# Sixty-six steps into fifty-nine: respacing the attention units of a two-layer encoder's second layer

## The chip, the core and the metric

The kernel runs on one core of a Trainium2 chip. A core has five engines that run side by side, each working through its own list of instructions in order: TensorE (PE in the profile, its weight loads as PEld), VectorE (DVE), ScalarE (ACT), GpSimd (POOL), and SyncE (SP), which here only issues DMA transfers. An instruction that needs another engine's result waits at the head of its engine's list, and all that is behind it in that list waits with it. The metric is the device time of one execution in microseconds (us); lower is better.

## What is computed

The input is `x` with 1024 rows of 1024 numbers. Two layers follow one another, and a last RMSNorm closes them. The change concerns the second layer only, differential attention with eight heads. Cut to what matters:

```python
def diff_mixer(h, ...):                       # h: 1024 x 1024, normalised rows of x
    q, k, v, gate = split(h @ w_in)           # w_in: 1024 x 4096
    # per head: q and k have 2 maps of 64, v has 128 columns
    sc = einsum('bqhcd,bkhcd->bhcqk', qb, k)  # two maps c = 0, 1
    p = softmax(sc - slopes * abs(pos_q - pos_k))
    a = p[:, :, 0] - lam * p[:, :, 1]
    o = rmsnorm(einsum('bhqk,bkhd->bqhd', a, v), head_g) * (1 - lambda_init)
    return (o * silu(gate)) @ w_o
```

All is float32. The kernel keeps that precision by splitting each operand of a product into a high and a low part in TensorE's faster float32 format; each product is then three matmuls (high by high, high by low, low by high).

## The kernel before

The second layer's attention is one loop, written out by hand: inside `tc.manual_schedule(engines=MAN)` the order of the program text is the order of every engine's list, so where a call stands in the loop decides what waits for what. Behind the loop, TensorE's and SyncE's lists stay in the text's order, and a scheduler orders the other three.

Two kinds of work are woven together in this loop.

- **Half blocks.** The projection `h @ w_in` is cut into blocks of 128 columns, named by kind and head: `V0`, `K1`, `Q1` and so on; a `G` block is a head's gate, a `W` block the V columns of two heads. `blocks` lists them in order. A block is worked off in halves of 512 rows (a `W` in four pieces); `block_mm` (lines 1156 to 1163) or `pair_mm` (1146 to 1154) issues a half's matmuls: 24 of 512 columns, or 48 of 256. Each half writes one PSUM tile `A`. Its copies out of PSUM are made by `DONE[kind]` in two portions, both taken up in the next step (`next(pend, 0)`): a high part on ACT (lines 97, 1177, 1215) and a low part on DVE (lines 1171, 1179, 1217 and 1218). A block's weights are loaded two blocks ahead, and split into high and low by a DVE cast (line 99) and a GpSimd subtraction (line 104).
- **Units.** A unit is one head and 128 of its query rows; there are 64, eight to a head. `scores` (line 1293) issues 12 matmuls into two PSUM tiles `S`, one for each softmax map. `maximum` (line 1299, on DVE) subtracts the distance bias, reads `S` for the last time and finds each row's maximum; `exp` (line 1307) runs on ACT; `ratio` and `combine` (lines 1311 to 1316, DVE) form the map `p`. One step later `transposes` (line 820) turns `p` on TensorE into two PSUM tiles `T`, and `split` copies these into a high part (line 97, ACT) and a low part (line 828, DVE). Each pair of units (a chunk) is then multiplied by V: `pv1`, 24 matmuls at line 1324, into a tile `A`. That product is copied to `ot` (line 1426, ACT), transposed into a tile `T` (`out1`, line 1330), copied from there and squared on ACT (lines 1331 and 1334).

PSUM is the scarce thing: there are two `S` tiles, two `T` tiles and two `A` tiles in all. One unit's scores fill both `S` tiles, so the next unit's scores cannot start before DVE has done both maxima of the unit before.

Each step of the loop runs in this order: scores of a new unit `nx`; the first portion of the last half block's copies; the unit's maxima and exponentials; the transposes and splits of the unit `cur` begun earlier; a half block; and then, where the step is in `DOUBLE`, a whole second unit, from scores to `combine`, with no half block behind it. Then come `out1`; up to four pieces of a head's finishing work on DVE (`finish1`: a reciprocal square root by steps on 128x8 tiles at lines 108 to 117, eight scalings at line 1348); a piece of the second layer's own modulation gate (`ada_gate`: DVE, lines 240 and 242; at its end TensorE, line 282); where the head's gate is done, `finish1b`, eight transposes at line 1358 into two `T` tiles and two DVE products at line 1360; the cast of the next block's weights; and last `pv1`, in every second step.

Before the change the loop has 66 steps, for u from -1 to 64. Each begins one unit, and those at u = 48, 51, 54 and 57 two. Each has a half block until these run out at u = 57. From u = 58 on there are units to finish and no half blocks, and in the same steps the loop loads and splits the weights of the output projection (`wo_split`: ACT high parts `woh`, GpSimd low parts `wol`) and the attention output of the first query half (`o_split`: ACT and DVE, tile `oT`); `WFILL` places output matmuls (`out_k`, lines 340 to 342) for row tiles 0 and 1 at u = 60, 61 and 62, two steps behind the splits that they need.

Of the kernel before, what the change touches and what calls it, by code (L numbers as in the profile page):

```python
# [55 lines left out]
def body(tc, x, c, positions, ada_w, ada_b, norm_g, mla_w_in, mla_q_norm_g, mla_w_q_up,  # L56
# [4 lines left out]
    with ctx:  # L61
# [1290 lines left out]
        def finish1b(h):  # L1352
# [19 lines left out]
            "V0 K1 Q1 W1 G0 K2 Q2 G1 K3 Q3 W3 G2 K4 Q4 G3 K5 Q5 W5 G4 K6 Q6 G5 K7 Q7 V7 G6 G7").split()]  # L1372
        NB = len(blocks)
        SKIP = ()
        stream, todo = {}, [(b, i) for b in range(NB) for i in range(4 if blocks[b][0] == "W" else 2)][1:]
        for u in range(-1, NU + 1):
            if u not in SKIP and todo:
                stream[u] = todo.pop(0)
# [17 lines left out]
        for u in range(-1, NU + 1):  # L1396
            n = 2 if u in DOUBLE else 1
            starts[u] = list(range(nu, nu + n))
            nu += n
        with tc.manual_schedule(engines=MAN):  # L1400
# [3 lines left out]
            for u in range(-1, NU + 1):  # L1404
                nxs = [units[v] for v in starts[u] if v < NU]
                for nx in nxs:
                    dist_load(nx.u + 2)
                b, hf = stream.get(u, (NB, 0))
                n = 4 if b < NB and blocks[b][0] == "W" else 2
                if hf == n - 1 and b + 2 < NB:  # L1410
                    kind, h = blocks[b + 2]
                    raws[b + 2] = pair_load(h) if kind == "W" else block_load(kind, h)
# [3 lines left out]
                if u < 0:  # L1416
# [4 lines left out]
                if u < 0:  # L1421
                    block_mm(ps, wq, 1, range(4, 8))
# [7 lines left out]
                cur = 0 <= u < NU  # L1430
                if cur:
                    tps = chunks[u // 2].transposes(units[u])
                for nx in nxs[:1]:
                    nx.maximum(1)
                    nx.exp(1)
                    if u < 0:
                        pend = q_done(heads[0], 1, ps)
                        next(pend)
# [3 lines left out]
                if cur:  # L1442
                    chunks[u // 2].split(units[u], tps)
                next(pend, 0)
                for k in WFILL.get(u, ()):
# [4 lines left out]
                blk = b < NB  # L1450
                if blk:
                    kind, h = blocks[b]
                    ps = A_()
                    if kind == "W":
                        pair_mm(ps, wb[b], hf)
                    else:
                        block_mm(ps, wb[b], hf, range(8))
# [13 lines left out]
                pump(fin, 4)  # L1471
                if u >= 8 and u % 2 == 0:
                    pump(gate1)
                if u in FIN:
                    pump(fin, 99)
                    finish1b(FIN[u])
                if blk:
                    pend = DONE[kind](heads[h], hf, ps)
                    if kind == "V":
                        turn = heads[h], hf  # L1480
                    if hf == n - 2 and b + 1 < NB:
                        wb[b + 1] = (pair_split if blocks[b + 1][0] == "W" else block_split)(raws[b + 1])
# [92 lines left out]
```

## Time and profile before

| | |
|---|---|
| three runs | 1637.22, 1638.22, 1638.44 us; median 1638.22 |
| profiled execution | 1639.5 us; its span, from the first to the last instruction, 1637.7 us |
| mean granted TensorE clock | 0.979 |
| busy in the span: PE, PEld, DVE, ACT, POOL | 1537.9, 1307.8, 1194.6, 814.0, 521.4 us |
| the second layer's scores start | from 891.9 to 1504.7 us of the span |

A busy TensorE in this profile is not TensorE at its peak, since matmuls overlap and their ends are modelled. The idle time in front of its instructions is what tells of waits, and the granted clock tells when the same matmuls run at half speed. The chain that ended last is of no help here (the page shows only the last 4 us of it), so the argument is read from stretches, waits and the timeline.

### The profile page before, as it was taken

The numbers are of one execution on the slowest core, as the hardware profiler recorded it, in microseconds if no ns is written. First come the engines' busy times: TensorE is split into PE (matmuls) and PEld (weight loads), VectorE is DVE, ScalarE is ACT, GpSimd is POOL, SyncE is SP. The second block draws the span as 40 slices with busy tenths as digits, with TensorE's granted clock in tenths as the row PEclk, the third lists the DMA queues.
The fourth block names the chain that finished last, engine by engine and source line by source line (L and its number), as shares of the span: only waits on it lengthen the run. The fifth ranks groups of instructions, "written<-read, shape, count | busy, mean of one in ns | idle before, by whom it ended". The sixth has DMA issues, their size and how long they took to land. (4 is left out here: it accounts for less than half of the span.)

```text
span 1637.7 us, 24634 instructions
## 1 busy us (share of the span) xinstructions
PE 1537.9 (94%) x9111; PEld 1307.8 (80%) x9111; DVE 1194.6 (73%) x2252; ACT 814.0 (50%) x1614; POOL 521.4 (32%) x486
## 2 busy tenths in 40 slices
PE   4788999999999999999999999999999999988897
PEld 3787778898888888887888898788877887766786
DVE  6866666888888888877445667777776677777764
ACT  6422115776777777786222444444544444445511
POOL 4444472453453453574253101110111011110422
PEclk8899999999999999999999999999999999999899
DMA  9007662110111111211234123333232223215122
GB/s 361 29 14 227 210 221 82 40 34 21 52 41 53 52 40 40 92 65 40 78 124 147 52 82 109 125 98 116 78 103 71 97 78 103 67 57 212 45 98 90
DMA packets 91583, 153.29 MB, mean 94 GB/s; under 512 B 5872, under 2 KB 60230, under 8 KB 91464
## 3 DMA queue, kind: packets, MB, share of 16 engines
q1 hardware_dynamic: 91464, 151.73, 27.9%
q8 instruction: 72, 1.18, 0.3%
q14 instruction: 47, 0.39, 0.1%
HBM read 126.01 MB, written 25.17 MB: 92 GB/s over the span
## 5 line engine op out<-in xcount | busy, mean ns | idle before, releaser
L828 DVE TENSOR_TENSOR ptl<-T,pth 128x512 fp32r<-128x512 f32 x384 | 246.0, 682 | 42.4 <-ACT pth L97 42.3
L97 ACT ACTIVATE pth<-T 128x512 fp32r<-128x512 f32 x384 | 207.2, 591 | 93.1 <-PE T L820 87.9
L104 POOL TENSOR_TENSOR wbl<-wblk,wbh 128x1024 fp32r<-128x1024 f32 x32 | 77.4, 2421 | 519.5 <-DVE wbh L99 277.6
L1299 DVE CUSTOM_DVE_ANT_0 p<-S,dist 128x1024 f32<-128x1024 f32 x128 | 156.1, 1219 | 114.5 <-PE S L1293 110.9
L1307 ACT ACTIVATE p<-p,m 128x1024 f32<-128x1024 f32 x128 | 147.6, 1153 | 173.8 <-DVE m L1301 153.3
L820 PE MATMUL T<-ident,p 128*128 128x128 f32 x1536 | 206.7, 277 | 5.4 <-DVE ptl L828 3.5
L820 PEld LDWEIGHTS T<-ident,p 128*128 128x128 f32 x1536 | 171.7, 141 | 42.3 <-issue 14.2
L856 POOL TENSOR_SCALAR p<-p,l 128x1024 f32<-128x1024 f32 x128 | 143.9, 1124 | 152.1 <-DVE l L855 104.5
L1159 PE MATMUL A<-hT,wbh 128*128 128x512 f32 x408 | 163.9, 402 | 0.0
L1160 PE MATMUL A<-hT,wbh 128*128 128x512 f32 x408 | 159.7, 391 | 0.0
L1161 PE MATMUL A<-hT,wbl 128*128 128x512 f32 x408 | 159.1, 390 | 0.0
L849 DVE TENSOR_REDUCE m<-S 128x1 f32<-128x1024 f32 x128 | 155.9, 1218 | 2.1 <-PE S L845 0.3
L854 ACT ACTIVATE p<-S,m 128x1024 f32<-128x1024 f32 x128 | 143.2, 1119 | 15.7 <-DVE m L849 10.3
L843 PE MATMUL S<-Kh,Q 96*128 96x512 f32 x256 | 108.5, 424 | 4.5 <-ACT p L854 2.6
L1293 PE MATMUL S<-KK,QQ 64*128 64x512 f32 x768 | 108.0, 412 | 1.9 <-DVE m L1299 1.9
L844 PE MATMUL S<-Kl,Q 96*128 96x512 f32 x256 | 100.5, 393 | 0.0
L845 PE MATMUL S<-Kh,Q 96*128 96x512 f32 x256 | 100.4, 392 | 0.0
L890 POOL TENSOR_TENSOR og<-ot,og 64x256 f32<-64x256 f32 x64 | 53.1, 829 | 130.9 <-DVE ot L889 128.7
L1161 PEld LDWEIGHTS A<-hT,wbl 128*128 128x128 f32 x408 | 76.8, 188 | 16.7
L1159 PEld LDWEIGHTS A<-hT,wbh 128*128 128x128 f32 x408 | 76.9, 189 | 15.1 <-issue 0.4
L340 PE MATMUL S<-woh,oT 128*128 128x512 f32 x224 | 88.7, 396 | 0.1
L1160 PEld LDWEIGHTS A<-hT,wbh 128*128 128x128 f32 x408 | 76.9, 188 | 14.4
(332 smaller groups left out, 3508.2 us busy)
## 6 DMA issues: line engine op xcount, KB each, us to landing
dist<-DD SPq DMA_DIRECT2D x64, 512.0 KB
adaw<-in_ada_w_dram SPq DMA_DIRECT2D x48, 512.0 KB
wblk<-in_diff_w_in_dram SPq DMA_DIRECT2D x32, 512.0 KB
qraw<-in_mla_w_q_up_dram SPq DMA_DIRECT2D x16, 288.0 KB
x<-in_x_dram SPq DMA_DIRECT2D x8, 512.0 KB
wraw<-in_mla_w_in_dram SPq DMA_DIRECT2D x8, 512.0 KB
OGD<-gt SPq DMA_DIRECT2D x8, 512.0 KB
Q<-RD SPq DMA_DIRECT2D x64, 64.0 KB
```

Source lines behind the costliest of these rows:

```text
L97: A.activation(o, i, AF.Copy)
L820: T.transpose(tp[:, i * P:(i + 1) * P], p[:, kt * P:(kt + 1) * P], ident)
L828: V.tensor_tensor(ptl[n][:, :, o], src, f(pth[n][:, :, o]), op=ALU.subtract)
L843: T.matmul(self.ps[:, n], q[:, 0, sl], Kh[b][:, kn], start=True, stop=False)
L849: V.tensor_reduce(self.m, self.ps, axis=AX.XY, op=ALU.max, negate=True)
L854: A.activation(p.rearrange("p (a b) -> p a b", b=512), self.ps, AF.Exp, bias=self.m, accum_out=l)
L856: G.tensor_scalar(p, p, l, 1.0, op0=ALU.mult, op1=ALU.mult)
L1159: T.matmul(ps, w[0][:, k], a, start=k == 0, stop=False)
L1160: T.matmul(ps, w[0][:, k], b, start=False, stop=False)
L1161: T.matmul(ps, w[1][:, k], a, start=False, stop=k == 7)
L1299: V.tensor_tensor_reduce(out=p, in0=self.ps[c_].rearrange("p a b -> p (a b)"), in1=dist[self.u], op0=ALU.subtract, op1=ALU.max, scale=1.0, ...
L1307: A.activation(p, p, AF.Exp, bias=self.m[c_], scale=2.0 ** -(self.h + 1), accum_out=L0[self.h][:, self.qt:self.qt + 1] if c_ == 0 else sel ...
```

## The change

The loop has 59 steps, s from -1 to 57, and each has a half block. Nine of them (s = 4, 11, 16, 23, 28, 35, 40, 47, 52) begin two units. In the step behind each of these two units are `cur`: the first one's transposes and split stay where they were, the second one's come at the end, behind the product with V. Each begun pair is an odd unit and the even one after it, so in the step that begins two units `cur` is an even unit, and no `pv1` stands in that step. The blocks are in another order: gates 0, 1 and 2 come later than before, and gates 3 to 7 are the last ten half blocks. A head's `finish1b` comes in the step behind its gate (s = 14, 28, 42, 50, 52, 54, 56; head 7's behind the loop). The last unit begins at s = 53. The output projection's splits are at s = 55, 56 and 57, and its matmuls inside the loop are those of k = 0 and 1 at s = 56, k = 2 and 3 at s = 57: one step behind their splits. Those of k = 4 and 5, for row tiles 0 and 1, come behind the loop. The matmuls are the same in number, 6474 rows of TensorE's list before and now.

```diff
-            "V0 K1 Q1 W1 G0 K2 Q2 G1 K3 Q3 W3 G2 K4 Q4 G3 K5 Q5 W5 G4 K6 Q6 G5 K7 Q7 V7 G6 G7").split()]
+            "V0 K1 Q1 W1 K2 Q2 G0 K3 Q3 W3 K4 Q4 G1 K5 Q5 W5 K6 Q6 G2 K7 Q7 V7 G3 G4 G5 G6 G7").split()]
...
-        WLOAD = {57: (0, 1), 58: (2, 3), 59: (4, 5), 60: (6, 7)}
-        WSPLIT = {58: (0, 1), 59: (2, 3), 60: (4, 5)}
-        WFILL = {60: (0, 1), 61: (2, 3), 62: (4, 5)}
-        OALLOC = {57: (0, 1), 59: (2, 3)}
-        DOUBLE = (48,51,54,57,)
-        FIN = {8 * h + 14: h for h in range(7)}
+        DOUBLE = (4, 11, 16, 23, 28, 35, 40, 47, 52)
         starts, nu = {}, 0
-        for u in range(-1, NU + 1):
-            n = 2 if u in DOUBLE else 1
-            starts[u] = list(range(nu, nu + n))
+        for s in range(-1, NS):
+            n = min(2 if s in DOUBLE else 1, NU - nu)
+            starts[s] = [units[v] for v in range(nu, nu + n)]
             nu += n
+        last = max(s for s in starts if starts[s])
+        FIN = {s + 1: blocks[b][1] for s, (b, i) in stream.items() if blocks[b][0] == "G" and i == 1 and s + 1 < NS}
+        WLOAD = {54: (0, 1), 55: (2, 3), 56: (4, 5), 57: (6, 7)}
+        WSPLIT = {55: (0, 1), 56: (2, 3), 57: (4, 5)}
+        WFILL = {56: (0, 1), 57: (2, 3)}
+        OALLOC = {54: (0,), 55: (1,), 56: (2,)}
...
-                if cur:
-                    tps = chunks[u // 2].transposes(units[u])
+                for c in curs[:1]:
+                    tps = chunks[c.u // 2].transposes(c)
...
-                pump(fin, 4)
-                if u >= 8 and u % 2 == 0:
+                pump(fin, 4 if s <= last + 2 else 99)
+                if any(c.u >= 8 and c.u % 2 == 0 for c in curs):
                     pump(gate1)
...
-                if cur and u % 2 == 1:
-                    acc = A_()
-                    pv1(acc, u // 8, chunks[u // 2])
-                    outs = u // 8, (u // 2) % 4, acc
-                if u >= 8 and u % 8 == 0:
-                    fin = finish1(u // 8 - 1)
+                for i, c in enumerate(curs):
+                    if i:
+                        chunks[c.u // 2].split(c, chunks[c.u // 2].transposes(c))
+                    if c.u % 2:
+                        acc = A_()
+                        pv1(acc, c.h, chunks[c.u // 2])
+                        outs = c.h, (c.u // 2) % 4, acc
+                    if c.u >= 8 and c.u % 8 == 0:
+                        fin = finish1(c.u // 8 - 1)
```

How this moves the lists is seen at three places. In the rows below `S`, `T` and `A` are the PSUM tiles with their numbers, `p` a unit's map, `KK` and `QQ` a head's keys and queries.

**TensorE, around the scores of unit 20.** Before, the last row of these scores, the unit before's transposes and a half block:

```order
L1293 MATMUL S_11251<-KK_10455,QQ_10757 128x512
L820 MATMUL T_11271<-ident,p_11168 128x128 x4
L820 MATMUL T_11276<-ident,p_11168 128x128 x4
L1159 MATMUL A_11295<-hT_9056,wbh_11035 128x512
L1160 MATMUL A_11295<-hT_9057,wbh_11035 128x512
L1161 MATMUL A_11295<-hT_9056,wbl_11036 128x512
```

Now, unit 20 is the second unit of s = 16:

```order
L1161 MATMUL A_11139<-hT_8726,wbl_10973 128x512
L1293 MATMUL S_11164<-KK_10330,QQ_10651 128x512
...
L1293 MATMUL S_11165<-KK_10330,QQ_10651 128x512
L1330 MATMUL T_11192<-ident,ot_11104 128x128 x2
L1293 MATMUL S_11217<-KK_10330,QQ_10651 128x512
L1293 MATMUL S_11218<-KK_10330,QQ_10651 128x512
```

The scores of unit 21 (`S_11217`, `S_11218`) stand right behind those of unit 20 (`S_11164`, `S_11165`), with the two transposes of `out1` between; the half block stands ahead of both.

**DVE, behind unit 20's `combine` (line 1316).** Before, the splits, four finishing pieces and the next unit's maximum:

```order
L1316 SCALAR_TENSOR_TENSOR p_11267<-p_11282,l_2142_11285,p_11267 128x1024
L828 TENSOR_TENSOR ptl_11193<-T_11271,pth_11192 128x4x128
L828 TENSOR_TENSOR ptl_11197<-T_11276,pth_11196 128x4x128
L113 TENSOR_TENSOR ort_11117<-ory_11118 128x8
L115 SCALAR_TENSOR_TENSOR ort_11117<-ort_11117,oms_11116 128x8
L117 SCALAR_TENSOR_TENSOR ory_11118<-ort_11117,ory_11118 128x8
L113 TENSOR_TENSOR ort_11117<-ory_11118 128x8
L1299 ISA p_11370,m_2150_11369<-S_11351,dist_11148 128x1024
```

Now:

```order
L1316 SCALAR_TENSOR_TENSOR p_11179<-p_11184,l_2126_11187,p_11179 128x1024
L110 TENSOR_SCALAR ory_11055<-ory_11055 128x8
L113 TENSOR_TENSOR ort_11054<-ory_11055 128x8
L115 SCALAR_TENSOR_TENSOR ort_11054<-ort_11054,oms_11053 128x8
L117 SCALAR_TENSOR_TENSOR ory_11055<-ort_11054,ory_11055 128x8
L242 SCALAR_TENSOR_TENSOR acc_10633<-adaw_10711,cT,acc_10633 128x1024
L99 CAST wbh_11205<-wblk_10978 128x1024
L99 CAST wbh_11209<-wblk_10980 128x1024
L1299 ISA p_11234,m_2138_11233<-S_11217,dist_11085 128x1024
```

Between unit 20's `combine` and unit 21's maximum stand the four finishing pieces, a piece of the modulation gate and two casts of a `W` block's weights; unit 20's splits have gone to the next step.

**TensorE, the first output matmuls of row tiles 0 and 1.** Before, these are behind the V product and the transposes of later units:

```order
L1324 MATMUL A_15560<-ptl_15509,V_2772_14964 128x256 x4
L820 MATMUL T_15611<-ident,p_15252 128x128 x4
L820 MATMUL T_15616<-ident,p_15252 128x128 x4
L340 MATMUL S_15629<-woh_15530,oT_15457 128x512
L341 MATMUL S_15629<-wol_15531,oT_15457 128x512
L342 MATMUL S_15629<-woh_15530,oT_15458 128x512
```

Now, at the start of s = 56:

```order
L1330 MATMUL T_15645<-ident,ot_15616 128x128 x2
L340 MATMUL S_15676<-woh_15661,oT_15612 128x512
L341 MATMUL S_15676<-wol_15662,oT_15612 128x512
L342 MATMUL S_15676<-woh_15661,oT_15613 128x512
```

They stand right behind the last `out1`, the one at the end of s = 55, with no V product and no transposes between.

More of the change, by code (lines that the diff above doesn't have):

```diff
@@ L1371, in body @@
         blocks = [(b[0], int(b[1])) for b in (
-            "V0 K1 Q1 W1 G0 K2 Q2 G1 K3 Q3 W3 G2 K4 Q4 G3 K5 Q5 W5 G4 K6 Q6 G5 K7 Q7 V7 G6 G7").split()]
+            "V0 K1 Q1 W1 K2 Q2 G0 K3 Q3 W3 K4 Q4 G1 K5 Q5 W5 K6 Q6 G2 K7 Q7 V7 G3 G4 G5 G6 G7").split()]
         NB = len(blocks)
-        SKIP = ()
-        stream, todo = {}, [(b, i) for b in range(NB) for i in range(4 if blocks[b][0] == "W" else 2)][1:]
-        for u in range(-1, NU + 1):
-            if u not in SKIP and todo:
-                stream[u] = todo.pop(0)
+        stream = [(b, i) for b in range(NB) for i in range(4 if blocks[b][0] == "W" else 2)][1:]
+        NS = len(stream) - 1
+        stream = {s: stream[s + 1] for s in range(-1, NS)}
         def dist_load(u):
@@ L1403, in body @@
             gate1 = ada_gate(1)
-            for u in range(-1, NU + 1):
-                nxs = [units[v] for v in starts[u] if v < NU]
+            for s in range(-1, NS):
+                nxs, curs = starts[s], starts.get(s - 1, [])
                 for nx in nxs:
                     dist_load(nx.u + 2)
-                b, hf = stream.get(u, (NB, 0))
-                n = 4 if b < NB and blocks[b][0] == "W" else 2
+                b, hf = stream[s]
+                kind, h = blocks[b]
+                n = 4 if kind == "W" else 2
                 if hf == n - 1 and b + 2 < NB:
-                    kind, h = blocks[b + 2]
-                    raws[b + 2] = pair_load(h) if kind == "W" else block_load(kind, h)
+                    k2, h2 = blocks[b + 2]
+                    raws[b + 2] = pair_load(h2) if k2 == "W" else block_load(k2, h2)
                 for nx in nxs:
@@ L1415, in body @@
                         O1[nx.h], SS[nx.h], L0[nx.h] = page((P, 8, P), name="o"), cl(8, "oss", 3), cl(8, "l0", 3)
-                if u < 0:
+                if s < 0:
                     ps = A_()
@@ L1420, in body @@
                     nx.scores()
-                if u < 0:
+                if s < 0:
                     block_mm(ps, wq, 1, range(4, 8))
@@ L1435, in body @@
                     nx.exp(1)
-                    if u < 0:
+                    if s < 0:
                         pend = q_done(heads[0], 1, ps)
@@ L1441, in body @@
                     nx.combine()
-                if cur:
-                    chunks[u // 2].split(units[u], tps)
+                for c in curs[:1]:
+                    chunks[c.u // 2].split(c, tps)
                 next(pend, 0)
-                for k in WFILL.get(u, ()):
+                for k in WFILL.get(s, ()):
                     if not part:
@@ L1449, in body @@
                         out_k(part[st], st, oT, wo, k)
[L1450 to L1457, printed above, removed]
+                ps = A_()
+                if kind == "W":
+                    pair_mm(ps, wb[b], hf)
+                else:
+                    block_mm(ps, wb[b], hf, range(8))
                 for nx in nxs[1:]:
```

47 lines of the change are left out of this document (26 added, 21 removed).

## The prediction, made before the changed kernel was run

> **What bounds the kernel now.** I read the stretches of the span first, to see where TensorE is the limit and where it is not, then the stretches in which its clock fell, then the timeline of single steps. The stretches are the steps with one unit each, the steps from the first double one (u = 48) on, the end of the attention, and the rest:
>
> ```profile
> 886.00:1384.00 498.00, 494.42 (x3146) 412.90 (x3145) 356.64 (x765) 231.20 (x497) 60.63 (x25) 1.00 0.29 94
> 1384.00:1504.00 120.00, 111.30 (x642) 88.02 (x642) 86.43 (x185) 56.39 (x116) 9.57 (x4) 0.96 0.33 115
> 1504.00:1563.00 59.00, 46.11 (x250) 38.41 (x247) 42.76 (x86) 29.92 (x65) 20.21 (x8) 0.88 0.17 63
> 1563.00:1638.00 75.00, 64.80 (x290) 53.43 (x288) 43.66 (x122) 11.45 (x21) 18.01 (x8) 0.95 0.25 92
> ```
>
> After the length come PE, PEld, DVE, ACT and POOL busy, the granted clock and DMA. In the first stretch TensorE is busy for 494.4 of 498 us at full clock, and DVE for 356.6: TensorE's work alone sets the pace, and nothing is to be had there. In the next two it is idle for 120 - 111.30 = 8.7 and 59 - 46.11 = 12.9 us, 21.6 in all, and its clock is below full. The clock was at half in three places:
>
> ```profile
> 1397.76:1401.17 3.41, 3.41 (x14) 0.50 0.00 0
> 1466.03:1472.86 6.83, 5.02 (x21) 0.50 0.22 76
> 1510.40:1524.05 13.65, 8.32 (x34) 0.50 0.00 0
> ```
>
> Here the columns are length, PE busy, clock and DMA. Half of the busy time is lost: (3.41 + 5.02 + 8.32) / 2 = 8.4 us. So the loop before loses 21.6 + 8.4 = **30.0 us** beyond TensorE's work, all of it from u = 48 on. The matmuls are the same before and now, so the change gains what it takes of these 30 us and pays what it adds.
>
> **What it removes.** All 30 us are at stake: the four old double steps and the steps at u = 58 to 64, where units are finished with no half block beside them. I credit the whole 30. What follows is what the new order loses in the same measure.
>
> **The nine double steps.** The step at u = 48, where `cur` is even, already has the order that the change makes nine times: scores, transposes, half block, scores, `out1`, and at once the next scores.
>
> ```profile
> 1392.15 1.66 PE L1293 MATMUL S<-KK,QQ 64*128 64x512 f32 x12
> 1393.74 0.44 PE L1330 MATMUL T<-ident,ot 128*128 128x128 f32 x2
> 1393.94 1.22 DVE L1299 CUSTOM_DVE_ANT_0 p<-S,dist 128x1024 f32<-128x1024 f32 x1 [1.18 <-issue]
> 1395.22 0.49 PE L1293 MATMUL S<-KK,QQ 64*128 64x512 f32 x1 [1.05 <-DVE m L1299]
> 1396.55 1.92 PE L1293 MATMUL S<-KK,QQ 64*128 64x512 f32 x11 [0.84 <-DVE m L1299]
> 1398.40 1.97 PE L820 MATMUL T<-ident,p 128*128 128x128 f32 x8
> 1398.70 0.19 ACT L1334 ACTIVATION_READ_ACCUMULATOR junk<-T 128x1 f32 x1
> 1400.02 0.77 PE L1159 MATMUL A<-hT,wbh 128*128 128x512 f32 x1
> 1406.10 2.08 PE L1324 MATMUL A<-pth,V 128*128 128x256 f32 x16
> 1417.20 0.44 PE L1330 MATMUL T<-ident,ot 128*128 128x128 f32 x2
> 1417.57 1.65 PE L1293 MATMUL S<-KK,QQ 64*128 64x512 f32 x12
> 1419.16 1.09 PE L820 MATMUL T<-ident,p 128*128 128x128 f32 x8
> 1420.01 0.49 PE L1159 MATMUL A<-hT,wbh 128*128 128x512 f32 x1
> 1425.68 1.66 PE L1293 MATMUL S<-KK,QQ 64*128 64x512 f32 x12
> ```
>
> A row is start, duration, engine, line and operation; the brackets hold the idle time before it and who ended it. The third unit's scores wait for the second's two maxima, which are 1.22 us each and can start only when the second's scores are complete: the first matmul waits 1.05 us, the rest another 0.84. Behind them the transposes need the `T` tile of `out1`, which ACT frees behind both exponentials, at 1398.70 + 0.19 = 1398.89. Without waits, `out1` takes 0.37 (1417.20 to 1417.57), scores 1.59 (to 1419.16), transposes 0.85 (to 1420.01) and a half block 5.67 (to 1425.68), so the half block would start 2.81 after 1393.74; it started 6.28 after. With slow matmuls inside it (1406.10 - 1400.02 = 6.08) this double step lost 3.5 + 0.4, some **4.0 us**. At full clock it would have lost less: both maxima end 2.8 us after the second scores (1396.55), the other 11 matmuls need 1.45, the first four transposes 0.42 and, from the `T` tile at 5.15, the last four 0.42: half block at 5.6, a loss of 2.8. Which of the two comes depends on the clock:
>
> ```profile
> 1394.35:1397.76 3.41, 1.70 (x11) 1.00 0.00 0
> 1438.72:1442.13 3.41, 1.76 (x14) 1.00 0.07 25
> ```
>
> ```profile
> 1440.37 0.44 PE L1330 MATMUL T<-ident,ot 128*128 128x128 f32 x2 [1.88 <-DVE ptl L828]
> ```
>
> In the 3.41 us ahead of the slow stretch TensorE was busy for 1.70 us; around the gap of 1.88 us ahead of 1440.37 it was busy for 1.76 and stayed at full clock. A double step's waits lie across 2.4 us, and all of them fall into one such stretch in about four cases of ten: (3.41 - 2.4) / 3.41 = 0.3, with some slack. I take 0.4: 2.8 + 0.4 x 1.2 = 3.3 each, nine times **29.5 us** (25.2 at full clock, 36 if all are slow).
>
> The Trainium skill, "TensorE: Matmul & The Clock Gate", section "Why this matters for your kernels", asks only for no idle gaps above about 3 us between bursts of matmuls. By that, gaps of 1.05 and 0.84 us would leave the clock alone, and the nine would lose 25.2 us in place of 29.5. This trace differs: two gaps of 1.9 us together went ahead of a clock of 0.50.
>
> **DVE behind the second unit.** Four of the nine have much DVE work between the second unit's `combine` and the next unit's maximum: it delays that unit's exponentials, and with these ACT's copy of `cur` (line 97), for which the V product in the next step waits. At u = 48 the work was one cast, and nothing waited:
>
> ```profile
> 1398.45 1.28 DVE L1316 SCALAR_TENSOR_TENSOR p<-p,l,p 128x1024 f32<-128x1024 f32 x1
> 1399.65 0.69 DVE L99 CAST wbh<-wblk 128x1024 fp32r<-128x1024 f32 x1
> 1400.25 1.22 DVE L1299 CUSTOM_DVE_ANT_0 p<-S,dist 128x1024 f32<-128x1024 f32 x1
> 1404.18 1.06 ACT L97 ACTIVATE pth<-T 128x512 fp32r<-128x512 f32 x2
> 1047.97 1.27 DVE L242 SCALAR_TENSOR_TENSOR acc<-adaw,cT,acc 128x1024 f32<-128x1024 f32 x1
> 1529.20 0.17 DVE L117 SCALAR_TENSOR_TENSOR ory<-ort,ory 128x8 f32<-128x8 f32 x1
> 1529.40 0.88 DVE L1348 TENSOR_SCALAR o<-o,ory 128x128 f32<-128x128 f32 x4
> ```
>
> With X for that work, and all times from the second scores' end: `combine` is over at 5.9, the maximum starts at 5.9 + X, and ACT's first copy starts 3.93 later (1400.25 to 1404.18) and takes about 0.53, so it is there at 10.4 + X. TensorE arrives after its half block, at 5.6 + 5.6 = 11.2 at full clock, or at 6.28 + 6.08 = 12.4 if slow. A small finishing piece takes 0.2, four scalings 0.9, the gate's piece 1.2, a cast 0.6. At s = 16 (the place in the order above) X = 0.8 + 1.2 + 1.2 = 3.2; at 11 and 23 it is 2.0, at 40 1.5, elsewhere small. The waits are 2.4 + 1.2 + 1.2 + 0.7 = 5.5 us if fast and 1.2 if slow; weighted, **3.8**.
>
> **Three double steps with more in them.** At s = 28 and 52 a head's `finish1b` stands between the second scores and the next ones, at 47 a V block's transposes (line 1190, as at u = 54). Both want `T` tiles that ACT frees only behind the second unit's exponentials. At u = 54 both stood there:
>
> ```profile
> 1462.68 0.38 PE L1330 MATMUL T<-ident,ot 128*128 128x128 f32 x2
> 1467.84 2.07 PE L1358 MATMUL T<-ident,o 128*128 128x128 f32 x8 [4.78 <-ACT junk L1334]
> 1469.84 2.93 PE L1293 MATMUL S<-KK,QQ 64*128 64x512 f32 x12
> ```
>
> 4.8 us of waiting and slow matmuls (2.07 for about 1.6, 2.93 for 1.65) make 6.5, or 3.2 above the plain 3.3. I take 3 for s = 52, 2 for 28, where the modulation gate's matmuls fill a part, and 1.3 for 47: **6.3 us** (0 to 9.6).
>
> **The end.** The output matmuls at s = 56 need the splits that s = 55 put at the end of ACT's list, behind the copies of the last `out1`. Before, a like chain ran from the `out1` at 1513.20:
>
> ```profile
> 1513.20 0.69 PE L1330 MATMUL T<-ident,ot 128*128 128x128 f32 x2 [7.13 <-DVE ptl L828]
> 1514.87 1.05 ACT L97 ACTIVATE woh<-woraw 128x1024 fp32r<-128x1024 f32 x1
> 1515.99 10.27 POOL L104 TENSOR_TENSOR wol<-woraw,woh 128x1024 fp32r<-128x1024 f32 x4 [42.16 <-ACT woh L97]
> 1516.46 5.22 DVE L104 TENSOR_TENSOR oT<-og,oT 128x512 fp32r<-128x512 f32 x2 [2.04 <-ACT oT L97]
> ```
>
> From `out1`'s start, `wol` of k = 0 is there at 2.79 + 10.27 / 4 = 5.4 and the low `oT`, 2.6 us beside GpSimd's work, at 3.26 + 2.61 = 5.9; k = 1's follow at 7.9 and 8.5. The last 10 of k = 1's 12 matmuls take 2.3, so the 24 end at 10.8 instead of 0.37 + 5.5 = 5.9: 5.0 lost, and after so long an idle time a slow stretch, as at 1510.40: 1.2 more. Before, u = 60's matmuls stood two steps behind their splits, and units' work covered this; that cover is what the change takes away. At s = 57 the low `oT` of k = 2 is behind `finish1b`'s two products on DVE: 1.2 to 3.5, I take 2.5. Behind the loop, row tile 2 needs the `A` tile of the last gate half, whose DVE portion stands behind eleven splits in its list: 1 to 4, I take 1.7. At s = 53 and 54 the transposes of units 62 and 63 are back to back and want four `T` tiles of two: a copy each, ACT 0.53 and DVE 0.68, 1.2. Sum **11.6 us** (6 to 15). DMA is no term: on SP a head's store still waits for `finish1b`'s product ahead of later distance loads, and these are issued at least one step before their unit.
>
> **Sum.** 29.5 + 3.8 + 6.3 + 11.6 = 51.2 us lost, against 30.0: 21 us slower. The profiled execution took 1639.5 us for its 1637.7 span, and the runs' median is 1638.2, so I forecast 1638.2 + 21 = **1659 us**. With each term at its low end: 25.2 + 5.5 + 0 + 6 = 36.7, or 1645; at its high end 36 + 1.2 + 9.6 + 15 = 62, or 1670.
>
> **Rivals.**
> *The pairs are covered: faster.* The second scores' wait vanishes where TensorE has other work behind them. At u = 51, `cur` being odd, a V product stood there:
>
> ```profile
> 1427.27 2.18 PE L1324 MATMUL A<-pth,V 128*128 128x256 f32 x16
> 1430.34 1.65 PE L1293 MATMUL S<-KK,QQ 64*128 64x512 f32 x12
> ```
>
> The scores at 1430.34 carry no idle time. If the new double steps were like this one, the first two terms would go, and 30.0 - 6.3 - 11.6 = 12 us would be won: 1626. Against it, the order shows only `out1` behind the second scores. It decides for faster once a pair costs under (30 - 18) / 9 = 1.3 us. Chance 0.07.
> *The waits only move: no change.* A pair that costs the two bare gaps, 1.9 us, with the end at 11.6 and the rest covered, loses 9 x 1.9 + 11.6 = 29: within a microsecond of 1638. It needs the `T` tile free early and a clock that never falls. Chance 0.08.
> *DVE becomes the bound.* If its lateness at one pair is still there at the next, each of the nine costs what u = 54 did: 9 x 6.5 + 11.6 = 70, or 1678. For it speaks DVE's share of 72% with one unit a step; against it, DVE had 141 us to spare in 498, and a pair comes only every five to seven steps. Chance 0.12.
> The forecast itself has 0.73.
>
> **Range and chances.** The forecast's own range is 1645 to 1670. With parts of the third rival above and some of the second below, 1643 to 1674 leaves out no more than 2 in 10. About 0.2%, or 3.3 us, is what a measurement of this kernel tells from no change: faster 0.07, within it 0.08, slower 0.85.
>
> **What would show it.** In the changed kernel's waits, TensorE's scores (line 1293) on DVE's maximum (line 1299) at nine places, some 17 us in all; its V product (1324) on ACT's copy (97) at s = 12, 17, 24 and 41; line 1358 on line 1334, and out1's 7 us wait gone; lines 341 and 342 on GpSimd and DVE before the first output matmuls, about 5 us. The granted clock would be below 1.00 in stretches of the steady part where it was 1.00. I am wrong if the scores at the nine places start without idle time, or if pairs cost their price but the end costs nothing.

## The result: slower by 1.5%

The changed kernel takes **1662.03 us** (median of four runs, 1661.3 to 1666.43) against 1638.33 before: 23.7 us more, a ratio of 1.015 with a 95% interval of 1.013 to 1.0169. A second measurement on another chip gave 1663.69 us and 1.0146 (1.0128 to 1.0164). The forecast was 1659.

The profiled execution took 1661.3 us, with a span of 1659.5. In the profile after, the stretches that answer to those shown of before (loop, end of the loop in two parts, rest) read:

```profile
889.00:1500.00 611.00, 585.18 (x3672) 483.66 (x3672) 437.63 (x949) 286.00 (x618) 64.70 (x27) 0.98 0.26 84
1500.00:1540.00 40.00, 31.93 (x173) 26.12 (x173) 20.28 (x42) 15.00 (x37) 6.75 (x3) 0.91 0.39 141
1540.00:1582.00 42.00, 36.04 (x149) 28.65 (x150) 32.55 (x49) 14.88 (x23) 16.84 (x7) 0.92 0.37 142
1582.00:1659.50 77.50, 67.91 (x300) 55.94 (x298) 41.21 (x118) 10.22 (x19) 18.01 (x8) 0.96 0.25 88
```

TensorE is idle for 25.8 us in the loop, where before it had lost 3.6 in the first 498, and for 8.1 and 6.0 at the end: 39.8 us. Up to 1582 us the clock was at half in eight places, of which the first and last and the sum are shown (length, PE busy, clock, DMA):

```profile
950.57:957.40 6.83, 6.57 (x29) 0.50 0.23 77
...
1571.80:1575.21 3.41, 3.41 (x9) 0.50 0.54 216
sum 37.54, PE 32.66; mean PE 4.08
```

Half of the busy 32.66 us is lost, 16.3. Together that is 56.2 us. Before, idle and clock came to 30.0 from u = 48 on, and to 33.6 with the 3.6 of the steady part. So the traces put the loss at 56.2 - 33.6 = 22.6 us, which is the medians' 23.7 within about a microsecond. Counted from the same instruction on (below), the two traces differ by 24.8 us; the 2 us that this sum lacks stand in the trace as TensorE's busy time, whose ends are modelled.

Who ended TensorE's idle time, summed over the loop and the end (engine, tile and line that waited, engine and line waited for: us, times, longest):

```profile
PE S L1293 <- DVE m L1299: 12.1, 14, 1.0
PE T L1358 <- ACT junk L1334: 6.0, 5, 4.3
PE A L282 <- ACT gate L283: 4.5, 1, 4.5
PE A L340 <- DVE GT L1218: 4.3, 1, 4.3
PE A L1324 <- ACT pth L97: 3.2, 2, 2.2
PE S L340 <- ACT oT L97: 2.6, 1, 2.6
...
PE S L341 <- POOL wol L104: 1.5, 1, 1.5
PE S L342 <- DVE oT L104: 1.1, 1, 1.1
```

Each line is one that the forecast had a term for: the score waits of the pairs, `finish1b`, the gate, the last `A` tile, the V product, the first output matmuls. The line left out is 1.5 us of transposes (line 820) that wait for a `T` tile. The 7.13 us wait of `out1` (line 1330) that stood at 1513.20 before is gone.

One caution for reading spans: the first layer varies from execution to execution. Unit 0's scores, ahead of which nothing was changed, start here at

```profile
888.90 0.50 PE L1293 MATMUL S<-KK,QQ 64*128 64x512 f32 x2
```

and in the trace of before at

```profile
891.86 0.50 PE L1293 MATMUL S<-KK,QQ 64*128 64x512 f32 x2
```

Below, "from unit 0" is a span less this start: 1659.5 - 888.90 = 770.6 us now, 1637.7 - 891.86 = 745.8 before. It compares two traces without the first layer.

### The profile page after: what moved, and what is told of

It reads as the page before. It is cut to its first block, busy times and chain, and to the rows that moved or that the text cites. A ratio compares the mean times of both kernels' runs of the same rounds, so it can differ in the third digit from the quotient of the medians.

```text
span 1659.5 us, 24631 instructions
## 1 busy us (share of the span) xinstructions
PE 1544.8 (93%) x9111; PEld 1310.5 (79%) x9111; DVE 1199.0 (72%) x2253; ACT 811.3 (49%) x1614; POOL 519.9 (31%) x485
## 5 line engine op out<-in xcount | busy, mean ns | idle before, releaser
L854 ACT ACTIVATE p<-S,m 128x1024 f32<-128x1024 f32 x128 | 143.1, 1118 | 15.7 <-DVE m L849 10.4
L1293 PE MATMUL S<-KK,QQ 64*128 64x512 f32 x768 | 114.8, 424 | 12.1 <-DVE m L1299 12.1
L1293 PEld LDWEIGHTS S<-KK,QQ 64*128 64x128 f32 x768 | 71.7, 193 | 38.8 <-DVE m L1299 15.9
L340 PE MATMUL S<-woh,oT 128*128 128x512 f32 x224 | 89.2, 398 | 2.7 <-ACT oT L97 2.6
L342 PE MATMUL S<-woh,oT 128*128 128x512 f32 x224 | 88.4, 395 | 1.1 <-DVE oT L104 1.1
```

The source lines that it names most:

```text
L854: A.activation(p.rearrange("p (a b) -> p a b", b=512), self.ps, AF.Exp, bias=self.m, accum_out=l)
L1293: T.matmul(self.ps[c_][:, n], q[r, zq, sl], k[zk][r, n * 512:(n + 1) * 512], start=i == 0, stop=i == 2)
```

## The experiments

All are edits of the changed kernel. Ratios are to the kernel before, run on the same chip.

### The double steps one step later

```diff
-        DOUBLE = (4, 11, 16, 23, 28, 35, 40, 47, 52)
+        DOUBLE = (5, 12, 17, 24, 29, 36, 41, 48, 53)
```

> All nine double steps one step later (5, 12, 17, 24, 29, 36, 41, 48, 53), where `cur` is odd, so that a V product of 2.1 to 3.0 us stands between the second unit's scores and the next unit's. Theory (the uncovered maxima behind the second scores are the cost of a pair): the idle time of the scores (L1293) on DVE's maximum (L1299), 12.1 us in the changed kernel, falls under 3 us and the clock stays at 1.00 at the plain pairs; the pairs cost 15 to 30 us less and the time is 1632 to 1648. Rival (the waits only move): the next step's two units are then finished back to back, their transposes and V product wait for ACT's copy, and the time stays at 1656 to 1666. Rival (DVE is the bound): no change of the time either, and DVE has no idle time at the pairs.

Measured: 1655.18 us, 1.0097 (1.0082 to 1.0112); from unit 0, 760.6 us. The largest wait:

```profile
PE T L1330 <- DVE ptl L828: 13.5, 8, 2.4
```

The score waits are gone, as the theory said, but the time is far from the theory's 1632 to 1648 and 0.8 us under the range of the rival by which the waits only move. They did move. With `cur` odd, the next step finishes two units and transposes both; `out1` needs a `T` tile that DVE frees with the low split of the first (line 828), and that split stands behind the third unit's maxima and `combine` in DVE's list. 13.5 us of new waits took the place of 12.1. That it is still 7 to 8 us under the changed kernel goes with other waits that shrank (line 1358 on ACT from 6.0 to 1.9 us, the gate from 4.5 to 0.8, the V product's 3.2 gone) and with a clock that fell in four stretches of the loop instead of six.

### The second unit's scores inside the half block

```diff
-                    block_mm(ps, wb[b], hf, range(8))
                 for nx in nxs[1:]:
-                    nx.scores()
+                        block_mm(ps, wb[b], hf, range(4))
+                        nx.scores()
+                        block_mm(ps, wb[b], hf, range(4, 8))
```

(and likewise for the two halves of a W pair; steps with one unit are as they were)

> Only the place of the second unit's scores changes: in the nine double steps they stand in the middle of the half block, so that its other half, some 2.8 us of matmuls, covers the second unit's maxima; the orders of DVE and ACT stay. Theory: of the 42.5 us that the pairs lose in the changed kernel's trace the score waits and the clock's falls beside them go, 20 to 30 us; V products that wait for ACT's copy at s = 12, 17, 24, 41, transposes that wait for a `T` tile and the two `finish1b` stay, so 1632 to 1642. Rival (the waits only move): DVE and ACT are late by the same amount behind the pair, and what the scores no longer wait the transposes and the V product wait: 1652 to 1662. Rival (DVE is the bound at a pair): nothing is won, 1660 to 1664.

Measured: 1651.3 us, 1.0073 (1.0058 to 1.0088); from unit 0, 756.7, 13.9 less. That lies between the theory and the rival, 0.7 us under the rival's 1652, and the waits say why:

```profile
PE A L1324 <- ACT pth L97: 4.9, 4, 2.3
PE T L1358 <- ACT junk L1334: 4.7, 5, 3.1
PE S L1293 <- DVE m L1299: 3.5, 7, 0.7
```

The score waits fell from 12.1 to 3.5 us, and of the pairs only those at s = 28, 47 and 52 had the clock fall. But the V product waits longer than before (3.2 to 4.9), because TensorE now gets there earlier while DVE's and ACT's lists are as they were. DVE's list at s = 16:

```profile
1086.05 1.28 DVE L1316 SCALAR_TENSOR_TENSOR p<-p,l,p 128x1024 f32<-128x1024 f32 x1
...
1087.93 1.28 DVE L242 SCALAR_TENSOR_TENSOR acc<-adaw,cT,acc 128x1024 f32<-128x1024 f32 x1
1089.13 1.29 DVE L99 CAST wbh<-wblk 128x1024 fp32r<-128x1024 f32 x2
1090.34 1.22 DVE L1299 CUSTOM_DVE_ANT_0 p<-S,dist 128x1024 f32<-128x1024 f32 x1
```

The third unit's maximum comes at 1090.34, behind the second's `combine`, the gate's piece and two casts. So covering TensorE's wait is half of it; the other half is the length of the chain through DVE and ACT.

### Finishing work and gate out of the double steps

```diff
+        FIN = {s + (s in DOUBLE): h for s, h in FIN.items()}
...
-                if any(c.u >= 8 and c.u % 2 == 0 for c in curs):
+                if any(c.u >= 8 and c.u % 2 == 0 for c in curs) and s not in DOUBLE:
```

> The two `finish1b` that fell on double steps (28 and 52) come one step later, and the modulation gate's pieces no longer run in double steps (so neither do its matmuls at s = 28 nor DVE's 1.27 us pieces at s = 11, 16, 23). Theory (terms b and c are caused by what stands in those steps): the gate's wait of 4.5 us (L282), most of the 6.0 us of L1358 on ACT's L1334 at s = 28 and 52, and the V product's 2.2 and 1.0 us at s = 17 and 24 go; some 6 to 9 us won, 1653 to 1657. Rival (they only hide the pair's own price, which then shows as a score wait and a `T` wait): 1659 to 1662.

Measured: 1661.66 us, 1.0136 (1.012 to 1.0152); from unit 0, 770.1 against 770.6. Nothing was won, and the theory's 1653 to 1657 is refuted, though the waits that it named did go:

```profile
PE S L1293 <- DVE m L1299: 15.8, 18, 1.0
...
PE T L1358 <- DVE ptl L828: 2.6, 5, 1.7
...
PE T L1358 <- ACT junk L1334: 1.6, 4, 0.7
```

The gate's wait fell from 4.5 to 0.7 us, `finish1b`'s on ACT from 6.0 to 1.6 (on DVE's line 828 it rose from 0.5 to 2.6), and the V product's from 3.2 to 1.2. The score waits now stand at all nine places (18 entries instead of 14), and the clock fell at all but one of the nine pairs, instead of six. Two things took the gain away. Counted from unit 0, the pair at s = 28 wins 3.8 us against the changed kernel, and behind s = 36 this is gone again. There the gate's matmuls now stand without a pair beside them:

```profile
1313.00 1.02 PE L282 MATMUL A<-acc,ones 128*128 128x512 f32 x2
1314.71 1.13 PE L282 MATMUL A<-acc,ones 128*128 128x512 f32 x2 [0.69 <-ACT gate L283]
```

The V product behind them starts at 1316.53, so the gate takes 3.5 us, which at s = 28 had overlapped the pair's own waits. And in both traces the V product did not wait where the clock had fallen in the pair, since the half block ahead of it then takes longer: the wait of 2.2 us at s = 17 and the slow matmuls are two prices for one lateness, of which one or the other was paid. At s = 17 and 24 together, waits gone and slow matmuls in their place, this run won 0.3 us.

### The end alone

```diff
-                for k in WFILL.get(s, ()):
...
                 ps = A_()
...
+                for k in WFILL.get(s, ()):
...
+                if s == NS - 1:
+                    for _ in pend:
+                        pass
```

> Only the end: at s = 56 and 57 the early output matmuls come behind the half block instead of ahead of it, and the last gate half's closing work on ACT and DVE comes ahead of the splits in their queues. Theory (the end's losses are the distance between a split and its matmuls, and a late `A` tile): the 4.1 us at s = 56, the 1.1 us at s = 57, the 4.35 us ahead of row tile 2 and the two falls of the clock beside them go, 10 to 13 us: 1649 to 1652. Rival (the splits on ACT, DVE and GpSimd set the end themselves): the waits come back at the next output matmuls behind the loop and the time is 1658 to 1662.

Measured: 1651.76 us, 1.0076 (1.006 to 1.0093); from unit 0, 757.7, so 12.9 less in the trace and 10.3 by the medians. The 4.1 us of waiting at s = 56 (2.6 and 1.5 in the list above), the 4.35 us ahead of row tile 2 and both falls of the clock are gone, and nothing came back behind the loop; the 1.1 us of line 342 stayed. What the late `A` tile was, the changed kernel's trace shows. TensorE first, then DVE:

```profile
1571.66 0.69 PE L340 MATMUL A<-woh,oT 128*128 128x512 f32 x1 [4.35 <-DVE GT L1218]
```

```profile
1567.40 2.48 DVE L104 TENSOR_TENSOR oT<-og,oT 128x512 fp32r<-128x512 f32 x4
...
1570.41 0.41 DVE L1217 TENSOR_SCALAR GT<-GT 128x512 f32<-128x512 f32 x1
1570.86 0.75 DVE L1218 SCALAR_TENSOR_TENSOR GT<-A,colsT,GT 128x512 f32<-128x512 f32 x1
```

The two short operations that free the tile stand behind all the splits.

### The second unit earlier on every engine

```diff
+                    if two:
+                        ps = A_()
+                        block_mm(ps, wb[b], hf, range(2)) if kind != "W" else pair_mm(ps, wb[b], hf, (0,))
+                        nxs[1].scores()
+                        nxs[1].maximum(0)
+                        chunks[curs[0].u // 2].split(curs[0], tps)
+                        nxs[1].exp(0)
+                        nxs[1].maximum(1)
+                        nxs[1].exp(1)
                     nx.ratio()
                     nx.combine()
+                    if two:
+                        nxs[1].ratio()
+                        nxs[1].combine()
```

(the rest of the half block follows; the old place of the second unit is empty)

> In the nine double steps the second unit's scores come behind a quarter of the half block (half of a W pair's), and on DVE its two maxima come ahead of the first unit's `combine` (line 1316), on ACT the copies of `cur` ahead of its exponentials. Theory after the run with the split half block (a pair's price is latency in DVE's and ACT's lists: there the second unit's maxima stood behind the first's `combine` and the work X behind them, so the third unit's were late by the same chain): with the chain shortened by some 3 to 4 us the waits of L1293 on L1299, of L1324 on L97 and of L1358 on L1334 fall to under 8 us together, the clock stays at 1.00 at the plain pairs, and 25 to 38 us of the 42.5 go: 1624 to 1637. Rival (DVE's amount of work at a pair, not its order, is the bound): as with the split half block, 1648 to 1653.

Measured: 1638.14 us, 0.9996 (0.9987 to 1.0006): 24 us less than the changed kernel, and no longer slower than before, but 1 us above the theory's 1624 to 1637. From unit 0, 743.8, 26.9 less than the changed kernel. A pair now reads so (s = 4):

```profile
940.71 1.65 PE L1293 MATMUL S<-KK,QQ 64*128 64x512 f32 x12
942.30 1.09 PE L820 MATMUL T<-ident,p 128*128 128x128 f32 x8
...
946.19 1.65 PE L1293 MATMUL S<-KK,QQ 64*128 64x512 f32 x12
...
951.05 0.49 PE L1293 MATMUL S<-KK,QQ 64*128 64x512 f32 x1
951.79 1.65 PE L1293 MATMUL S<-KK,QQ 64*128 64x512 f32 x11 [0.25 <-DVE m L1299]
```

The half block's rows between 942.30 and 946.19, and behind 946.19 with those of `out1`, are left out. The third unit's scores wait for 0.25 us where they waited for 0.95 + 0.83. The two kernels with early scores differ most where the forecast had put its extra price. Taking the start of a row behind each pair in each trace against the changed kernel's, counted from unit 0, the pairs at s = 28, 47 and 52 win 4.9, 2.5 and 4.1 us here, and won 2.0, 0.3 and 0.5 with the split half block; the other six win 1.2 to 4.2 here and 1.1 to 4.1 there. At those three, `finish1b`, the gate and `v_turn` want tiles that ACT frees behind the second unit's exponentials, so the orders on ACT and DVE decided there. This run changes both, and TensorE's as well; no run takes them apart. The V product's wait stayed:

```profile
PE A L1324 <- ACT pth L97: 3.9, 4, 2.0
```

### Filling the wait with work that is thrown away

```diff
-            for j in range(2):
+            for j in list(range(2)) * again:
                 T.transpose(tp[:, j * P:(j + 1) * P], t[:, j * P:(j + 1) * P], ident)
...
-                    out1(outs[0], outs[1], t)
+                    out1(outs[0], outs[1], t, 5 if s in DOUBLE else 1)
```

> The transposes of `out1` are issued five times in place of once in the nine double steps (8 more of 128x128, some 0.85 us), the same result written again, so that TensorE works through most of the 0.95 us in which it waits for the second unit's first maximum; nothing else changes. Theory (the clock falls because a pair's two waits leave TensorE too little busy in one stretch of 3.41 us): the work is hidden in the wait, the stretches at half clock at s = 4, 11, 35, 40 go, 1.2 to 1.7 us each: 1653 to 1658. Rival (the clock falls for another reason, or the pair's price at full clock is the same): 1660 to 1664.

Measured: 1664.24 us (1659.69 to 1666.33), 1.0152 (1.0131 to 1.0172): no gain by the times, so the theory's 1653 to 1658 is missed. Its profiled execution, the fastest of the four with 1659.69 us, does show the mechanism. The 3.41 us stretch around the pair at s = 4 (length, PE busy, clock):

```profile
951.03:954.44 3.41, 2.50 (x19) 1.00 0.00 0
```

TensorE works through 2.5 us of it, as of the one at s = 35, and among the pairs the clock falls at s = 28 and 52 alone. From unit 0 this execution takes 765.4 us, 5.2 less than the changed kernel. The other three took 1662.69 to 1666.33, and their granted clocks on record are lower too: 0.977 to 0.978 for the whole execution against 0.982. So eight extra transposes are not shown to keep the clock up in every execution, and the median does not test what a fall costs; where the clock fell in those three, no trace shows.

### The changed kernel once more, and half the filling

```diff
-                    out1(outs[0], outs[1], t)
+                    out1(outs[0], outs[1], t, 3 if s in DOUBLE else 1)
```

> The changed kernel again, unedited, on the chip of the next one. Theory and rival alike: 1660 to 1666.

> As e6_fill, but with four more transposes in the nine double steps instead of eight (some 0.43 us instead of 0.85). In the profile of e6_fill the falls of the clock at s = 4, 11, 35 and 40 were gone and the stretch from 889 us on was 6 us shorter, but its times (1664.24) were not. Theory (the clock's fall costs time and filling the wait prevents it): 3 to 6 us under the changed kernel on the same chip, with a clock of 0.978 or more against 0.976. Rival (which executions have the clock fall at which pair is chance, and what it costs at one pair a V product's wait costs where it does not fall): within 2 us of it.

Measured, on one chip: the changed kernel 1663.69 us, 1.0146 (1.0128 to 1.0164); with four extra transposes 1664.08 us, 1.0148 (1.0132 to 1.0164). No difference, as the rival said; but the clock, 0.976 to 0.977, did not reach the theory's 0.978 either, and in the profiled execution it fell at six pairs as without them, so this run does not test the cost of a fall. The two executions of the unedited kernel do. Of the stretches around a pair, the first had these at s = 4 and 16:

```profile
947.16:950.57 3.41, 1.89 (x13) 1.00 0.00 0
...
1083.69:1087.11 3.42, 2.33 (x15) 1.00 0.55 153
```

The clock was at 0.50 in the stretch behind the first, and stayed at 1.00 behind the second. In the second execution, s = 4 and 16 read:

```profile
950.21:953.62 3.41, 2.09 (x15) 1.00 0.00 0
...
1096.98:1100.39 3.41, 1.20 (x10) 1.00 0.47 154
```

There it fell behind the second, which holds the V product's wait of 2.21 us behind this pair, and not behind the first. The falls were at s = 4, 11, 28, 35, 40 and 52 in one execution and at 16, 23, 28, 35, 47 and 52 in the other, and from unit 0 the two differ by 0.3 us (770.6 and 770.3). That the sums agree does not mean that a fall is free. These are the scores of s = 6, in the first execution and then in the second:

```profile
965.91 0.51 PE L1293 MATMUL S<-KK,QQ 64*128 64x512 f32 x2
```

```profile
966.56 0.50 PE L1293 MATMUL S<-KK,QQ 64*128 64x512 f32 x2
```

They come 965.91 - 888.90 = 77.0 us behind unit 0's where the clock had fallen at s = 4, and 966.56 - 892.14 = 74.4 where it had not: this fall cost 2.6 us. Read in the same way, the others that only one execution had cost 1.2 (s = 16), 0.7 (s = 47), 0.3 (s = 40) and nothing at s = 11 and 23, where the V product waits for 1.0 us if the clock does not fall, and not at all if it does. Where the falls lie differs between executions; that they cost about the same in sum in these two is chance.

### The double steps two steps apart

```diff
-        DOUBLE = (4, 11, 16, 23, 28, 35, 40, 47, 52)
+        DOUBLE = (36, 38, 40, 42, 44, 46, 48, 50, 52)
...
+                        pump(fin, 99)
                         fin = finish1(c.u // 8 - 1)
```

> The nine double steps are not spread but stand two steps apart, at s = 36, 38, ... 52; the order of the half blocks stays the changed kernel's. Theory (a pair costs its latency, and what it leaves late on DVE is made good in one plain step): about the same price for each, 1658 to 1670. Rival (DVE becomes the bound: three units in two steps are more than DVE can do, and its lateness adds up): 1675 to 1700.

Measured: 1670.37 us, 1.0193 (1.0177 to 1.0208), 7 to 8 us more than spread (1663.69 and 1662.03), 0.4 us past the theory's upper edge and well short of the rival's 1675 to 1700. The stretch that holds all nine pairs:

```profile
1275.00:1520.00 245.00, 218.97 (x1241) 175.30 (x1242) 172.81 (x383) 114.37 (x249) 21.60 (x9) 0.92 0.22 71
```

DVE, the third number of busy time, works 172.8 of 245 us, 71%, even here, and ACT 47%: neither is the bound. The largest single wait is `finish1b`'s for a `T` tile,

```profile
PE T L1358 <- ACT junk L1334: 14.1, 6, 4.3
```

12.8 of it in three waits in this stretch, since three heads' ends now fall on double steps (s = 42, 50 and 52) where two did.

### Early second unit and new end together

```diff
+                        nxs[1].scores()
+                        nxs[1].maximum(0)
...
+                    block_mm(ps, wb[b], hf, range(2, 8) if two else range(8))
                 for k in WFILL.get(s, ()):
...
+                if s == NS - 1:
+                    for _ in pend:
+                        pass
```

> The early second scores of e5_early and the new order at the end of e4_end together. Theory (the two losses are separate): what each wins by itself adds up, 10 us under e5_early's time, 1613 to 1627, faster than the kernel before the change. Rival (the end only looks late because the steps ahead of it are): within 3 us of e5_early.

Measured: **1624.68 us**, 0.9911 (0.9894 to 0.9927): 0.9% faster than the kernel before, and 37 us under the change. From unit 0 it is 731.1, which is 12.7 us under the early second unit alone, and the end alone had won 12.9, so the two losses are separate and add up. The stretches of this kernel that answer to the changed kernel's:

```profile
892.00:1480.00 588.00, 578.37 (x3681) 479.14 (x3682) 437.72 (x953) 288.54 (x626) 65.03 (x27) 1.00 0.27 87
1480.00:1520.00 40.00, 37.26 (x206) 31.06 (x205) 23.07 (x39) 16.23 (x34) 11.39 (x5) 1.00 0.51 191
1520.00:1546.00 26.00, 24.93 (x118) 20.52 (x117) 25.45 (x45) 10.52 (x17) 12.36 (x5) 1.00 0.40 153
```

TensorE is busy for 98% of the loop, at full clock but for one stretch of 3.41 us, and for 25 of the last 26 us.

### And the finishing work moved as well

To the edits of the kernel above:

```diff
+        FIN = {s + (s in DOUBLE): h for s, h in FIN.items()}
...
+                if any(c.u >= 8 and c.u % 2 == 0 for c in curs) and s not in DOUBLE:
```

> e8_both with the two edits of e3_move added: `finish1b` one step later where it fell on a double step, and no gate piece in a double step. Alone on the changed kernel these two won nothing measurable (1661.66 against 1662.03). Theory (there the removed V product waits and `T` waits were replaced by falls of the clock, because the score waits stood beside them; with the score waits gone they are the last waits): the V product's 2.0, 0.7 and 0.8 us at s = 17, 12 and 24 and the 1.1 us of L1358 at s = 52 go, 3 to 6 us: 1619 to 1622. Rival (these edits only shift work to steps that pay the same): 1623 to 1626.

Measured: 1624.73 us, 0.9912 (0.9897 to 0.9927): the same; from unit 0, 729.9 against 731.1. The theory's first half held: the V product's waits on line 97 fell from 3.8 to 1.2 us, and counted from unit 0 the scores behind s = 28 start 5.9 us earlier than without these edits (a part of it is a fall of the clock that the other execution had behind s = 16). Behind s = 36, where the gate's matmuls now stand as in the run with these edits alone, 3.7 us of this are lost again. But `finish1b`, one step later at s = 53, now stands right behind the half block and waits there for the low split of `cur`:

```profile
1486.75 1.91 PE L1358 MATMUL T<-ident,o 128*128 128x128 f32 x8 [2.59 <-DVE ptl L828]
```

That is another 1.0 us, and 1.2 are left in the trace. The rival holds: most of the work pays where it now stands.

## Why the prediction was right, point by point

**Bound and credit.** That TensorE's work sets the pace and that the change plays for 30 us of idle time and slow clock held as far as it could be seen: with both losses cut (the early second unit and the new end) the new order beats the old one by 14 us, with TensorE busy for 98% of its loop and 13.4 us of idle time left in the three stretches shown. That all 30 us are won was credited, and no run shows it.

**The nine double steps (29.5 us).** Right in mechanism and, at full clock, in size; the price of a slow stretch was off both ways. The pair at s = 16, from `out1` on:

```profile
1085.10 0.44 PE L1330 MATMUL T<-ident,ot 128*128 128x128 f32 x2
1086.49 0.49 PE L1293 MATMUL S<-KK,QQ 64*128 64x512 f32 x1 [0.95 <-DVE m L1299]
1087.81 1.65 PE L1293 MATMUL S<-KK,QQ 64*128 64x512 f32 x11 [0.83 <-DVE m L1299]
...
1090.20 0.66 PE L820 MATMUL T<-ident,p 128*128 128x128 f32 x4 [0.16 <-ACT junk L1334]
1090.61 0.48 PE L1159 MATMUL A<-hT,wbh 128*128 128x512 f32 x1
```

From `out1` to the half block 1090.61 - 1085.10 = 5.51 us, where 2.81 are needed: 2.7 lost, against the 2.8 forecast. At s = 4 with the clock at half it is 955.31 - 948.11 = 7.20, so 4.4 lost, and 0.9 more in the half block's first matmuls, which are still slow: 5.3 against the 4.0 forecast. The chance of a slow stretch was put too low: it came at four of the seven plain pairs in one execution and at four in the other, not at 0.4 of them. What it adds to a pair was put at 1.2 us everywhere, and was 0 to 2.6 at the six places where the two executions differ, 0.8 in the mean. The two errors nearly cancel, which is luck. Of the score waits some 17 us at nine places were announced; 12.1 at seven came, since at s = 28 and 52 longer waits stood ahead of them.

Here the trace goes against the Trainium skill, "TensorE: Matmul & The Clock Gate", section "Why this matters for your kernels", which asks only for no idle gap above about 3 us: two gaps of under 1 us each went ahead of falls to 0.50. By that rule the nine would have lost 25.2 us; in the trace the clock fell at six of them, with 12.9 us lost at half speed, which that sum lacks. That the busy share of a stretch of 3.41 us at full clock counts is what the stretches around the pairs show, in every profile of this study (up to 1.70 us busy, then 0.50; from 2.09 us on, 1.00; in between, both). It is no sharp rule: at the end of the loop one such stretch of the changed kernel (1534.28 to 1537.69) had 1.65 us of busy time, and the next stayed at 1.00. That this share, moved by itself, changes the median was not shown.

**DVE behind the second unit (3.8 us).** Right: the V product waited for 2.22 us at s = 17 (2.4 forecast) and 1.02 at s = 24 (1.2), and not at s = 12 and 41, where the clock had fallen, as the two cases said. The sum was 3.2, and the two executions show why slow pairs must not be charged twice: at s = 11 and 23 the time came out the same with the fall as with the wait.

**`finish1b`, gate and `v_turn` (6.3 us).** About the right size, for partly the wrong reason. `finish1b` at s = 52 waited 4.34 us, against 4.78 at u = 54. But at s = 28 the forecast let the gate's matmuls fill a part of the wait, and they were what waited:

```profile
1225.99 2.08 PE L282 MATMUL A<-acc,ones 128*128 128x512 f32 x2 [4.46 <-ACT gate L283]
```

```profile
1225.34 0.60 ACT L283 ACTIVATE gate<-A 128x512 f32<-128x512 f32 x1
```

They want the `A` tile of the gate's first two matmuls (at 1220.51), which ACT copies at 1225.34, behind the second unit's exponentials in its list. And the forecast added this term to a plain pair's price, as if the work could be moved away and its price with it; the run with this work moved shows that the two overlap: 3.8 us were won behind s = 28 and paid again at s = 36.

**The end (11.6 us).** Right in mechanism; in size right by the medians and 2.5 us short by the trace: the run with the end alone, which takes out all of it but the step at s = 53 and 54, won 12.9 us in the trace and 10.3 by the medians, against 11.6 - 1.2 = 10.4 (and left 1.1 us of the wait at s = 57 in place). The term that was mis-sized is the last gate half's `A` tile: 1.7 us taken, bounds 1 to 4, measured 4.35 of waiting and a slow stretch behind it (1571.80 to 1575.21, half of 3.41), 6.1 together. The splits at s = 56 were nearer: 2.59 + 1.48 of waiting and 1.7 of slow matmuls against 6.2, and 1.08 at s = 57 against 2.5.

**Sum.** 51.2 us lost against 30.0 was forecast, 21 us; the traces have 56.2 against 33.6, both with the small gaps of the steady part, 22.6; the medians 23.7. The pairs' three terms make 39.6 of it, and the early second unit took back 24 us of these by the medians; with the new end 37 us of the loss are undone by edits, the rest is read from the waits alone.

**The rivals.** *The pairs are covered* did not come, since nothing stood behind the second scores. Its price of 1626 with the end as it is was not reached either: with the second unit early on all three engines and the old end the time was 1638, and it took the new end as well to be faster. Its own cover, a V product behind the second scores, is not enough: the shifted double steps had that and stayed at 1.0097. *The waits only move: no change* asked for two bare gaps of 1.9 us and a clock that never falls; the pair at s = 16 lost 2.7, and the clock fell at six pairs. *DVE becomes the bound* fell: 71% busy with the pairs two steps apart, and 7 to 8 us more, not 16 or more.

## What to carry to other kernels

When two units of a software pipeline start in one step, look at how long the chain of the first runs through the slower engines before the second's first operation gets its turn; covering the matmul engine's wait alone moves the wait to the next tile that the same chain frees (13.5 us for 12.1 here) and won 7 to 11 us. Put the second unit's first operations ahead of the first's last ones in every list: that was worth 24 us, moving the side work to other steps nothing. And let the short operation that frees an accumulator stand ahead of long splits in the list: two operations of 0.41 and 0.75 us, standing behind the splits, held TensorE for 4.35.

## What was unexpected of the hardware

Two executions of one program had the clock fall at different pairs (s = 4, 11, 40 in one, 16, 23, 47 in the other) and yet took the same time from unit 0 on, within 0.3 us. Each fall had its own price all the same: 2.6 us at s = 4, nothing at s = 11 and 23, where a wait that the fall replaces costs as much. Four extra transposes in the wait did not keep the clock up at s = 16, 23, 35 and 47; eight did in the one execution profiled, which was the fastest of its four and the one with the highest clock. So one trace is one draw: where the clock falls is to be compared over several executions before a median is explained by it.
